# A hybrid decoder step on one core: the closing stage of each 512-token segment gets a rank 800 operations later

## The chip, the core and the metric

The kernel runs on one core of a Trainium2 chip. A core has a matrix engine (TensorE, PE), a vector engine (VectorE, DVE), a scalar engine (ScalarE, ACT), a general engine (GpSimd, POOL) and a queue engine (SyncE, SP). Each works through its own list of instructions in order. Instructions of different engines wait for each other by semaphores. The metric is the device time of one execution in microseconds (us), the median of several runs.

## The reference

One layer of a causal decoder runs over a prompt of 2048 tokens (width 1024) and over a sample batch of 8 sequences of 4 tokens. In short:

```
u    = x * (1 + scale) + shift                 # from the conditioning vector
proj = u @ w_in                                # 9344 columns
A    = rwkv7(proj)                             # 16 heads of 64: a delta-rule recurrence
B    = retention(proj)                         # 4 heads, chunks of 128 tokens
merged = sigmoid(g_a) * o_a + sigmoid(g_b) * o_b
sub  = merged @ w_out
y    = norm(alpha * x + gate * sub) * ln_gain + ln_bias
```

The last line is the closing stage that the change moves.

## The kernel before, in words

The prompt is cut into four segments of 512 tokens. In each segment the kernel goes over four retention heads, and with each head over two pairs of recurrence heads. `run` records the work of a head by a list of steps (`ORDER`): `P0` and `P1` are the projections of a pair, `G0` and `G1` the gate projections, `R` the projections and `S` the arithmetic of the retention head, `J` prepares half a pair and runs `solve`, `N` and `M` merge, `O` is the output projection of the head before, and `D` is the decode of the sample batch, which runs once, in segment 2. A projection is 24 matmuls of 128 x 512 into a PSUM tile `pp` (three of them). Its weights are a 1 MB tile `ww` (three of them), a high and a low part side by side, which POOL loads from a copy in DRAM (`wc_wf`) that segment 0 wrote. `solve` is a chain: it inverts a matrix in six levels (DVE writes `HH` and two copies `bdH`, PE multiplies), and then walks four chunks of the recurrence.

The step `O` of a segment's first head also closes the segment before: its fourth head is projected, and then `final` runs on the finished tile `zt` (128 x 4 x 1024, one buffer). `final` is 76 operations: for each of two column halves a DMA of the gate row and for each of four row blocks a DMA of x, a POOL multiplication by the gate, a DVE addition and a DVE statistic; then the row statistics (a POOL power among them); then for each half two DMAs (gain and bias rows) and for each block a DVE normalization, a POOL multiplication, a DVE addition and the DMA to the output. Its DMAs are issued by SP into four `fx` tiles. The last segment does not come here (`outproj_last`), so `final` runs three times for the prompt, in segments 1, 2 and 3. A fourth call, for the sample batch, is small and stands elsewhere.

Nothing of this is issued as recorded. `Plan` records every operation with a number, finds what each depends on, and `schedule` then plays the whole list through a cost model of the five engines: at each step the engine that is free first takes, of its operations that are ready, the one with the lowest rank. The rank is the recorded number plus an offset that holds while the operation is recorded:

```
op.num = len(self.ops)
op.prio = op.num + self.prio_off
```

PE chooses among ranks less than 500 apart (`WIN`); weights tiles keep their order. An operation is never held back for its rank: where an engine has nothing else ready, it takes it. The first work of a segment (`uprep`) already has an offset, -700. The result is a fixed list for each engine.

All instructions of the trace carry line 529, where recorded operations are issued, so they are told apart by tile names.

Of the kernel before, what the change touches and what calls it, by code (L numbers as in the profile page):

```python
# [62 lines left out]
RUN = 2  # L63
UPO = 700
DOFF = 0
JBN = 3, 2, 2, 2, 2
JB=dict(zip(("AR", "W", "UV", "BT", "Z"), JBN))
NPP,NSM = 3,3
# [758 lines left out]
class Mixer:  # L827
# [980 lines left out]
    def outproj(self, s, h, dec):  # L1808
        T, V, A, G = self.T, self.V, self.A, self.G
        last = s == self.ns - 1  # L1810
        if last and h == NH_B - 1:
            return self.outproj_last(s)
        if h == 0:
            self.zt = self.j1.tile([128, 4, D], F32, tag="zt", name="zt")
        for q in range(4):
            qs = slice(q * 256, (q + 1) * 256)
            if last:
                if q % 2 == 0:
                    wg = self.ww.tile([128, 2, 2, 512], F32R, tag="ww", name="ww")
                hi, lo = self.split(self.i["wo"][h, q], wg[:, q % 2, 0], wg[:, q % 2, 1], gate=q)  # L1820
            else:
                if q % 2 == 0:
                    wp = self.wpair("wo", (h, q), [self.i["wo"][h, q + g] for g in range(2)], s < self.ns - 2)
                hi, lo = wp[q % 2]
            ws = [slice(k * 256, (k + 1) * 256) for k in range(2)]
            for i2 in range(2):
                pz = self.pp.tile([128, 2, 256], F32, tag="pp", name="pp")
                for j in range(2):
                    i = i2 * 2 + j
                    n = 0  # L1830
                    for k in (1, 0):
                        mh, ml = self.mg[k]
                        for w, m in ((hi, mh), (hi, ml), (lo, mh)):
                            T.matmul(pz[:, j], lhsT=m[:, i * 128:(i + 1) * 128], rhs=w[:, ws[k]], start=n == 0, stop=n == 5)
                            n += 1
                z = self.zt[:, 2 * i2:2 * i2 + 2, qs]
                if h == 0 and last:
                    x = self.fx((128, 2, 256))
                    r = s * SEG + i2 * 256
                    self.nc.sync.dma_start(out=x, in_=self.i["xp"][r:r + 256, qs].rearrange("(j p) c -> p j c", j=2))  # L1840
                    V.scalar_tensor_tensor(out=z, in0=x, scalar=ALPHA, in1=pz, op0=MUL, op1=ADD)
                elif h == 0:
                    A.copy(out=z, in_=pz)
                else:
                    V.tensor_tensor(out=z, in0=pz, in1=z, op=ADD)
            if dec:
                self.outproj_dec(h, [(q, (hi, lo))])
        self.mg = {}
        if h == NH_B - 1:
            rows = [slice(s * SEG + i * 128, s * SEG + (i + 1) * 128) for i in range(4)]  # L1850
            self.final([[self.zt[:, i, 0:512], self.zt[:, i, 512:1024]] for i in range(4)], 128,
                       [self.i["xp"][r] for r in rows], [self.o["yp"][r] for r in rows], False)

    def outproj_last(self, s):

# [108 lines left out]
    def run(self):  # L1964
# [3 lines left out]
        for s in range(self.ns):  # L1968
# [8 lines left out]
            for h in range(NH_B):  # L1977
                last = s == self.ns - 1 and h == NH_B - 1
                gate = {}
                for step in (LAST if last else ORDER if s + h else BEGIN).split():  # L1980
# [28 lines left out]
                    elif step[0] == "D" and s == self.dseg + 1 and h == 0:  # L2009
                        self.pl.prio_off = DOFF  # L2010
                        self.decode()
# [28 lines left out]
```

## Time and profile before

| what | value |
| --- | --- |
| median of 3 runs | 3134.05 us (3130.12 to 3137.01) |
| the profiled execution, its own time | 3128.51 us |
| its span, first to last instruction | 3126.7 us |
| PE busy | 2896.4 us, 93% of the span |
| DVE, ACT, POOL busy | 61%, 50%, 34% |
| mean granted PE clock | 0.969 of full |

The profiled execution lies 5.5 us under the median. PE is the engine that is busy nearly all the time, so the end of the program moves by what PE waits, by what its clock loses, and by little else. A row of the timeline gives the start, the length, the engine, the operation, out<-in by names, the shape and a count of equal instructions in a row; in brackets stands how long the engine was idle before, and what ended that.

### The profile page before, as it was taken

Reading aid. Unit: us, or ns where it says so; the run is one execution under the profiler, and the core shown is the slowest. Engines: PE = TensorE matmul, PEld = TensorE weight load, DVE = VectorE, ACT = ScalarE, POOL = GpSimd, SP = SyncE. Lnnn points to the kernel's source line nnn. Section 1 sums busy time; section 2 is a strip of 40 time slices with the busy share of each in tenths; the row PEclk is TensorE's granted clock in tenths of the full one; section 3 lists DMA queues with packets and bytes.
Section 4 is the critical chain, followed back from the end, with each engine's and each line's share of the span. In section 5 each row is a group of like instructions: output and inputs, shape, how many; then the busy total and the mean of one; then the engine's idle time right before and its main releaser. Section 6 shows DMA issues by size and latency. Waiting matters only on the chain. (4 is left out here: it accounts for less than half of the span.)

```text
span 3126.7 us, 63842 instructions
## 1 busy us (share of the span) xinstructions
PE 2896.4 (93%) x24700; PEld 2332.8 (75%) x24700; DVE 1919.9 (61%) x4748; ACT 1566.2 (50%) x3859; POOL 1048.3 (34%) x1451
## 2 busy tenths in 40 slices
PE   8999999989989999989998788999999989998996
PEld 5777778768888989879774466777787766777675
DVE  3566676666576365565665575565676675566666
ACT  4466755656436455453541045554555346454652
POOL 4554456433252131222210242232232442334232
PEclk9999999999999999999998789999999999999997
DMA  8564556534362433425344432333343452533321
GB/s 303 199 229 161 175 191 222 191 127 160 117 226 99 130 108 112 137 94 178 136 128 150 158 110 97 135 124 122 131 152 124 156 176 79 172 119 122 108 83 38
DMA packets 132792, 451.86 MB, mean 145 GB/s; under 512 B 30500, under 2 KB 41636, under 8 KB 92680
## 3 DMA queue, kind: packets, MB, share of 16 engines
q0 software_dynamic: 33120, 241.19, 22.5%
q1 hardware_dynamic: 99368, 206.58, 19.6%
q8 instruction: 195, 3.19, 0.4%
q14 instruction: 109, 0.89, 0.1%
HBM read 345.83 MB, written 101.88 MB: 143 GB/s over the span
## 5 line engine op out<-in xcount | busy, mean ns | idle before, releaser
L529 PE MATMUL pp<-uh,ww 128*128 128x512 f32 (+1 forms) x5152 | 1476.8, 366 | 43.8 <-DMA ww<-wc_wf 15.6
L529 PEld LDWEIGHTS pp<-uh,ww 128*128 128x128 f32 x5152 | 880.5, 190 | 168.3 <-DVE t L529 22.7
L529 PE MATMUL pp<-ul,ww 128*128 128x512 f32 (+1 forms) x2576 | 883.7, 364 | 0.1
L529 PEld LDWEIGHTS pp<-ul,ww 128*128 128x128 f32 x2576 | 468.6, 190 | 54.5 <-issue 1.4
L529 POOL DMA_DIRECT2D ww<-wc_wf x190 | 109.0, 574 | 625.3 <-PE pp L529 514.5
L529 POOL TENSOR_TENSOR ww<-fx,ww 128x512 fp32r<-128x512 f32 x178 | 234.4, 1330 | 211.5 <-ACT ww L529 197.7
L529 ACT CAST ZX<-sm 128x512 f16<-128x512 f32 (+1 forms) x363 | 206.3, 572 | 91.0 <-PE sm L529 86.7
L529 ACT ACTIVATE tn<-UV,PL 64x64 f32<-64x64 f32 x512 | 177.0, 346 | 117.9 <-DVE UV L529 95.8
L529 POOL TENSOR_TENSOR t<-t,t 128x256 fp32r<-128x256 f32 (+2 forms) x160 | 150.6, 943 | 199.5 <-ACT t L529 189.1
L529 DVE TENSOR_TENSOR HH<-sm,lev 128x512 f16<-128x512 f32 (+1 forms) x165 | 111.3, 674 | 160.5 <-PE sm L529 159.7
L529 PE MATMUL pp<-ww,mh 128*128 128x256 f32 x960 | 190.4, 290 | 3.5 <-ACT zt L529 1.9
L529 DVE TENSOR_SCALAR UV<-ch 64x64 f32<-64x64 f32 x256 | 55.2, 227 | 207.3 <-ACT UV L529 184.4
L529 POOL TENSOR_TENSOR tn<-tn,mhalf 128x4 f32<-128x4 f32 (+2 forms) x108 | 100.9, 935 | 216.1 <-DVE tn L529 214.1
L529 PE MATMUL pp<-ww,uh 128*128 128x256 f32 x1024 | 171.6, 291 | 1.4 <-DVE t L529 0.8
L529 ACT CAST bdZ<-sm 64x512 f16<-64x512 f32 (+1 forms) x264 | 149.5, 566 | 24.9 <-PE sm L529 20.1
L529 PEld LDWEIGHTS pp<-ww,mh 128*128 128x128 f32 x960 | 154.9, 193 | 8.0 <-ACT zt L529 2.3
L529 PEld LDWEIGHTS pp<-ww,uh 128*128 128x128 f32 x1024 | 140.7, 190 | 5.3 <-ACT UV L529 0.7
L529 DVE SCALAR_TENSOR_TENSOR UV<-ch,PL,tn 64x64 f32<-64x64 f32 x384 | 108.7, 283 | 57.4 <-PE ch L529 47.5
L529 ACT ACTIVATE t<-pp 128x512 f32<-128x512 f32 (+1 forms) x160 | 80.6, 519 | 118.3 <-PE pp L529 100.7
L529 PE MATMUL pp<-ww,ml 128*128 128x256 f32 x480 | 138.4, 289 | 0.1
L529 ACT ACTIVATE UV<-ch 64x64 f32<-64x64 f32 x256 | 51.6, 215 | 171.3 <-PE yy L529 137.8
L529 DVE COPY bdH<-HH 64x512 f16<-64x512 f16 (+1 forms) x396 | 124.7, 315 | 8.5
(255 smaller groups left out, 5420.1 us busy)
## 6 DMA issues: line engine op xcount, KB each, us to landing
ww<-wc_wf POOLq DMA_DIRECT2D x190, 1024.0 KB, 5.1
wc_wf<-ww SPq DMA_DIRECT2D x65, 1024.0 KB, 5.4
fx<-in_wf SPq DMA_DIRECT2D x140, 256.0 KB, 3.4
ww<-wc_wv POOLq DMA_DIRECT2D x24, 1024.0 KB, 5.2
ww<-wc_wo POOLq DMA_DIRECT2D x16, 1024.0 KB, 5.1
wa<-in_wa SPq DMA_DIRECT2D x16, 512.0 KB, 5.2
wc_wv<-ww SPq DMA_DIRECT2D x8, 1024.0 KB, 5.5
fx<-in_wo SPq DMA_DIRECT2D x32, 256.0 KB, 2.8
```

What stands on the lines that cost most here:

```text
L529: op.fn = lambda: real(*[res(x) for x in a], **{k: res(x) for k, x in kw.items()})
```

## The change

The three calls of `final` for the prompt are recorded with an offset of +800, so each of their operations ranks like one recorded 800 operations later. The operations themselves, their tiles and what they depend on stay as they are.

```diff
@@ -63,6 +63,7 @@
 RUN = 2
 UPO = 700
 DOFF = 0
+FOFF = 800
 JBN = 3, 2, 2, 2, 2
@@ -1848,8 +1849,10 @@
         self.mg = {}
         if h == NH_B - 1:
             rows = [slice(s * SEG + i * 128, s * SEG + (i + 1) * 128) for i in range(4)]
+            off, self.pl.prio_off = self.pl.prio_off, FOFF
             self.final([[self.zt[:, i, 0:512], self.zt[:, i, 512:1024]] for i in range(4)], 128,
                        [self.i["xp"][r] for r in rows], [self.o["yp"][r] for r in rows], False)
+            self.pl.prio_off = off
```

Recorded 800 operations later stand the rest of the first head's steps (`G1`, `S`, `J`, `M`) and the first steps of the second head. The lists of the five engines are the same before and after up to each `final`, differ for some 200 to 350 us of work around it, and are the same again before the next one. The added line moves every line number by one.

On DVE in segment 1, after the statistics of `final`. Before, the rows with `zt` and `fx` or `tn` are `final`; `AR` and `BK` are a pair's preparation, and `t<-pp,omu,t` empties a projection's PSUM tile:

```order
L529 TENSOR_TENSOR AR<-t_10662,t_11273 128x4x64
L529 TENSOR_SCALAR zt<-zt,tn 128x512 x3
L529 TENSOR_TENSOR zt<-zt,fx 128x512 x3
L529 TENSOR_SCALAR zt<-zt,tn 128x512 x3
L529 TENSOR_TENSOR zt<-zt,fx 128x512 x3
L529 TENSOR_SCALAR zt<-zt,tn 128x512 x2
L529 TENSOR_TENSOR AR<-t_10575,t_11273 128x4x64
L529 SCALAR_TENSOR_TENSOR t_11409<-pp,omu,t_11342 128x256 x2
```

After, the same stretch, from the same first row to the emptying of the same tile:

```order
L530 TENSOR_TENSOR AR<-t_10662,t_11293 128x4x64
L530 BN_STATS tn<-zt 128x6
L530 BN_AGGR tn<-tn 128x2
L530 TENSOR_TENSOR AR<-t_10575,t_11293 128x4x64
L530 SCALAR_TENSOR_TENSOR t_11340<-t_11213,t_10662 128x256
L530 BN_AGGR tn<-tn 128x2
L530 SCALAR_TENSOR_TENSOR t_11351<-t_11232,t_10662 128x256
L530 SCALAR_TENSOR_TENSOR BK<-t_11340,t_11298 64x4x64 x2
L530 SCALAR_TENSOR_TENSOR t_11382<-pp,omu,t_11337 128x256 x2
```

Fourteen rows' worth of normalizations and additions stood between the two `AR` and ahead of the emptying; now three short statistics stand there.

On POOL in segment 2, behind the decode. Before; `lw` is the pair of small weights that the next pair's first matmuls read, and `zt<-zt,fx` are `final`'s gate multiplications:

```order
L529 DMA ww<-wc_wv_0_2375 128x2048
L529 TENSOR_TENSOR zt<-zt,fx 128x512 x4
L529 COPY PL<-t_22078 128x4
L529 TENSOR_SCALAR t_22113<-t_22016 128x4x64
L529 TENSOR_SCALAR t_22122<-t_22017,hka,oka 128x256
L529 MEMSET t_22113 128x4
L529 TENSOR_TENSOR t_22122<-t_22122,t_20456 128x256
L529 TENSOR_TENSOR lw<-t_22084,lw 128x256
```

After:

```order
L530 TENSOR_TENSOR t_22014<-t_22014,t_20456 128x256
L530 TENSOR_TENSOR zt<-zt,fx 128x512
L530 TENSOR_TENSOR tn<-tn,mhalf 128x2
L530 COPY PL<-t_22054 128x4
L530 TENSOR_TENSOR lw<-t_21992,lw 128x256
L530 TENSOR_TENSOR tn<-tn,mhalf 128x2
L530 TENSOR_SCALAR t_22091<-t_22060 128x4x64
```

`lw` now stands ahead of the second half's four multiplications and of the other half pair's operations, with one multiplication in front of it.

On POOL in segment 3, where it issues the loads of projection weights (`DMA ww<-wc_wf`, the number names the block). Before:

```order
L529 DMA ww<-wc_wf_2062 128x2048
L529 TENSOR_TENSOR tn<-tn,mhalf 128x4
L529 TENSOR_TENSOR zt<-zt,fx 128x512 x3
L529 COPY t_30476<-carry 128x1
L529 COPY t_30510<-carry 128x1
L529 COPY carry<-t_30476 128x1
L529 COPY carry<-t_30510 128x1
L529 TENSOR_TENSOR zt<-zt,fx 128x512 x4
L529 DMA ww<-wc_wf_2131 128x2048
L529 DMA ww<-wc_wf_2170 128x2048
```

After:

```order
L530 DMA ww<-wc_wf_2062 128x2048
L530 TENSOR_TENSOR zt<-zt,fx 128x512 x3
L530 TENSOR_TENSOR t_30469<-t_30392,t_30460 128x256
L530 COPY t_30473<-carry 128x1
L530 DMA ww<-wc_wf_2131 128x2048
L530 TENSOR_TENSOR bdL<-W,B_29946 64x4x64 x2
L530 TENSOR_SCALAR t_30515<-t_30490 128x4x64
```

Between the loads of blocks 2062 and 2131 stood seven multiplications and the power (`tn<-tn,mhalf`, which waits for the row statistics); now three multiplications of the first pass stand there.

## Rows read from the trace of the kernel before

**Rows 1.** The page: span, and busy time by engine

```profile
span 3126.7 us, 63842 instructions
PE 2896.4 (93%) x24700; PEld 2332.8 (75%) x24700; DVE 1919.9 (61%) x4748; ACT 1566.2 (50%) x3859; POOL 1048.3 (34%) x1451
```

**Rows 2.** Instructions on the tile zt: count, ns min/median/max, first and last start

```profile
L529 POOL TENSOR_TENSOR zt<-zt,fx x48: 1257/1461/2487, 876.1 to 2521.0; 128x512 f32<-128x512 f32 x48
L529 DVE BATCH_NORM_STATS2 tn<-zt x32: 632/682/695, 878.8 to 3117.2; 128x6 f32<-128x512 f32 x32
...
L529 DVE SCALAR_TENSOR_TENSOR zt<-fx,zt x24: 633/692/1780, 877.4 to 2501.5; 128x512 f32<-128x512 f32 x24
L529 DVE TENSOR_SCALAR zt<-zt,tn x24: 529/663/1519, 900.2 to 2520.4; 128x512 f32<-128x512 f32 x24
L529 DVE TENSOR_TENSOR zt<-zt,fx x24: 678/1384/1785, 903.0 to 2523.7; 128x512 f32<-128x512 f32 x24
```

**Rows 3.** Stretches: length, busy PE, PEld, DVE, ACT, POOL, clock, DMA share, GB/s

```profile
890.00:921.00 31.00, 19.09 (x136) 18.70 (x137) 29.11 (x46) 7.35 (x21) 24.03 (x27) 0.83 0.68 237
921.00:970.00 49.00, 46.02 (x542) 41.23 (x542) 30.94 (x75) 30.23 (x77) 10.99 (x18) 1.00 0.43 144
...
1784.00:1831.00 47.00, 27.25 (x143) 20.74 (x141) 40.85 (x66) 14.56 (x28) 35.87 (x36) 0.75 0.52 167
1831.00:1880.00 49.00, 45.01 (x470) 35.91 (x467) 28.74 (x86) 30.69 (x81) 9.17 (x16) 0.97 0.28 97
...
2471.00:2527.00 56.00, 41.60 (x197) 33.87 (x195) 45.35 (x65) 8.81 (x18) 37.73 (x39) 0.92 0.69 224
2527.00:2580.00 53.00, 50.90 (x502) 41.77 (x502) 31.27 (x69) 28.08 (x61) 11.51 (x18) 0.96 0.42 149
```

**Rows 4.** Timeline of PE: its long waits in the three stretches

```profile
917.04 0.59 PE L529 MATMUL pp<-uh,ww 128*128 128x272 f32 x1 [10.23 <-DVE t L529]
...
1787.20 0.39 PE L529 MATMUL sm<-lora,lw 128*128 128x256 f32 x1 [2.60 <-ACT lw L529]
1795.92 1.01 PE L529 MATMUL sm<-lora,lw 128*128 128x256 f32 x3 [8.33 <-POOL lw L529]
...
1818.15 0.73 PE L529 MATMUL pp<-uh,ww 128*128 128x512 f32 x1 [5.00 <-DVE gate_t L529]
...
2491.25 0.77 PE L529 MATMUL pp<-uh,ww 128*128 128x512 f32 x1 [3.45 <-DMA ww<-wc_wf]
...
2526.93 0.77 PE L529 MATMUL pp<-uh,ww 128*128 128x512 f32 x1 [9.33 <-DMA ww<-wc_wf]
```

**Rows 5.** Timeline of DVE in segment 1; last row: inside a solve

```profile
899.61 0.41 DVE L529 TENSOR_TENSOR AR<-t,t 128x256 f32<-128x256 f32 x1
900.25 2.66 DVE L529 TENSOR_SCALAR zt<-zt,tn 128x512 f32<-128x512 f32 x3 [0.23 <-POOL tn L529]
...
915.10 1.48 DVE L529 TENSOR_TENSOR AR<-t,t 128x256 f32<-128x256 f32 x1
916.51 1.26 DVE L529 SCALAR_TENSOR_TENSOR t<-pp,omu,t 128x256 f32<-128x256 f32 x3
...
942.32 0.69 DVE L529 TENSOR_TENSOR HH<-sm,lev 128x512 f16<-128x512 f32 x1 [1.34 <-PE sm L529]
```

**Rows 6.** Timeline of POOL in segments 2 and 3

```profile
1785.56 6.85 POOL L529 TENSOR_TENSOR zt<-zt,fx 128x512 f32<-128x512 f32 x4
...
1794.69 1.17 POOL L529 TENSOR_TENSOR lw<-t,lw 128x256 fp32r<-128x256 f32 x1
...
2476.85 6.14 POOL L529 TENSOR_TENSOR zt<-zt,fx 128x512 f32<-128x512 f32 x4 [3.87 <-DMA fx<-gdram]
...
2512.62 6.07 POOL L529 TENSOR_TENSOR zt<-zt,fx 128x512 f32<-128x512 f32 x4
2518.64 1.71 POOL L529 DMA_DIRECT2D ww<-wc_wf  x3
```

**Rows 7.** Stretch behind the first long wait, columns as in rows 3

```profile
917.00:921.00 4.00, 3.96 (x19) 3.96 (x20) 3.91 (x10) 1.63 (x2) 1.31 (x2) 0.56 0.48 145
```

## The prediction

> **What bounds the kernel now.** I read the page first: PE is busy for 2896.4 of 3126.7 us, so 230 us of idle PE are all that an order of work can win back, apart from its clock [rows 1]. The reader is to see there which engine decides, and that the others have room on average. Then I looked for where `final` runs, by its tile [rows 2]: 48 POOL multiplications are three stages of 16, and the 24 of each kind on DVE are three times 8. By medians a stage is 16 x 1.46 = 23.4 us of POOL and 8 x (0.69 + 0.66 + 1.38 + 0.68) = 27.3 us of DVE, with five small DVE instructions more. Third, the stretches in which it runs [rows 3]: there DVE is busy for 29.11 of 31, 40.85 of 47 and 45.35 of 56 us, and PE stands idle for 11.9, 19.8 and 14.4 us, 46 us together. In the stretches right behind them DVE has 18.1, 20.3 and 21.7 us free and PE idles for only 3.0, 4.0 and 2.1 us. So the average of 61% for DVE hides three places where DVE and POOL are the bound, and there the last thing that PE waits for is read one wait at a time [rows 4].
>
> **The waits, each with what stood ahead of its releaser.** In segment 1 PE waits 10.23 us for `t`, the emptying of a PSUM tile. DVE reaches it at 916.51; from 900.25 to 915.10 it runs fourteen instructions of `final`, then one `AR` [rows 5]. In segment 2 PE waits 2.60 us for one half of `lw`, 8.33 us for the other and 5.00 us for `gate_t`, another emptying [rows 4]. POOL writes `lw` at 1794.69, behind four multiplications that begin at 1785.56 and take 6.85 us and behind a few instructions of the pair [rows 6]; `gate_t` stands behind instructions of `final` on DVE in the same way. In segment 3 PE waits 3.45 and 9.33 us for weights [rows 4]. Their loads are issued by POOL in its order: the load that PE lacks at 2526.93 is one of three issued at 2518.64, right behind four multiplications of 6.07 us, and the earlier one stood behind four of 6.14 us which had themselves waited 3.87 us for the gate row [rows 6]. Sum of the six waits: 10.23 + 2.60 + 8.33 + 5.00 + 3.45 + 9.33 = 38.9 us.
>
> **The change part by part.** It adds and removes no instruction; it moves three times 76.
>
> First, what leaves its place ahead of the releasers. The order shows it at each of them. In segment 1 the emptying has no normalization ahead of it any more. PE had stopped 10.23 us before 917.04, so at 906.8; without the fourteen instructions DVE, at 900 where it was before, has the statistics, one `AR`, two short products and two `BK` to do, an estimate of 3.5 us if each takes up to twice the 0.41 us of the `AR` [rows 5], and reaches the emptying before PE needs it. I take the whole 10.2 us. In segment 2 `lw` has one multiplication ahead of it in place of four and no longer the other half pair, and no instruction of the additions of `final` stands ahead of `gate_t`. I take 8.3 + 5.0 us as gone, and leave the 2.6 us, since what PE comes to next there (transposes of the retention output) waits for a POOL power and four DVE instructions; since that may cost 1.4 us more, I count 12 us. In segment 3 the load of block 2131 has three multiplications (4.4 us) ahead of it in place of seven and a power. PE does not outrun that by more than a little, so I leave 2 us and count 10.8 us. Together 10.2 + 12 + 10.8 = 33 us. The bounds are 0, if other work on the same engines is as late, and 46 us, the whole idle time of the stretches.
>
> Second, the clock. After the wait of 10.23 us PE runs for 4 us at a mean clock of 0.56, so at the lower of its two levels, 1.2 of 2.4 GHz, for most of it, and loses 3.96 x 0.44 = 1.7 us [rows 7]. Three of the waits are of this kind, one in each segment, so 5 us come back with them; bounds 0 and 10.
>
> Third, what is given back where the 76 operations go. The normalizations now stand between the instructions of `solve`: by the order, 14 of the 37 DVE instructions of the first stage, 31 of the second and 29 of the third stand behind the start of the first solve. That is 74 x (27.3 / 37 = 0.74) = 55 us, against 60 us of free DVE in the three stretches behind [rows 3]. Where DVE waits for PE between two levels, 1.34 us, one of them fits without delay [rows 5]; where it falls between `HH` and its copies it lengthens the chain by its own 0.7 to 1.4 us. The cover is PE's own projection matmuls, which fill the chain's gaps (3 us idle of 49 in such a stretch [rows 3]); if that cover is gone, the chain's delay is PE's. The bounds are 0 and 55. I take 8 us: about a third of the 55 us on the chain, and less than half of that seen by PE. The solve itself also begins earlier, because the `AR` and `BK` that it needs are no longer behind `final`, which speaks for the lower end.
>
> Fourth, the rest. SP issues the same 22 DMAs a stage in nearly the same places, so its queue is not moved past anything that PE reads. The `fx` tiles are held longer, but no other user of them is near; the one `zt` is wanted again only by the second head's output projection. On both I put 0 to 3 us and take 0. The rows of the lists that differ elsewhere are neighbours exchanged; 0 with 4 us to either side.
>
> Sum: 3128.5 - 33 - 5 + 8 = 3098.5 us against the profiled execution's own time. This lies 5.5 us under the median of the runs, so the median I predict is 3104 us, 30 us less than before.
>
> One row and one rule speak against it. `AR<-t,t` took 0.41 us at 899.61, and 1.48 us at 915.10 with a multiplication of POOL beside it [rows 5]; `zt<-zt,fx` on DVE goes from 0.68 to 1.79 us [rows 2]. The Trainium skill (SBUF — State Buffer, section Who interferes with whom) says that a VectorE instruction with two inputs in SBUF, or a copy in a two-port mode, and a GpSimd instruction exclude each other for the whole instruction, whichever came first. By it the multiplications, now among the copies of the solve, would each hold one link of the chain for 1.46 us; the trace agrees as far as these two rows go. That is the first rival.
>
> **The rivals.**
> 1. The shared access gives back half. With about ten of the 16 multiplications of each stage behind the start of a solve, 30 x 1.46 = 44 us can fall on links of the chain; if half does and PE sees half again to two thirds of it, 11 to 15 us come back beyond my 8, and the time is 3115 to 3127 us. For it: the stretched rows above. Against it: in the old place the two engines met too, 29 of 31 us busy DVE beside 24 us of POOL [rows 3].
> 2. The waits only change their name: PE lacks PSUM tiles or weights for another reason at the same place, such as the pair's own chain behind the decode, and 3134 us stay, within 6 us. For it: the stretch behind the decode has a low clock, 0.75 [rows 3], so PE is short of work there. Against it: in segments 1 and 3 there is nothing else between the releaser and its data.
> 3. Slower: the solve chain becomes PE's bound. Its place is the first solve behind each stage, its price the 55 us of DVE instructions now inside. It decides from the point where PE sees more than 38 of them, that is when the projections run out in all three solves; with all 55 seen, the time is 3134 + 17 = 3151 us. For it: 31 and 29 of 37 instructions stand there. Against it: 60 us of free DVE, and the schedule's preference for the chain wherever both are ready.
>
> **How the numbers follow.** The forecast, 3092 to 3116 us: 0.62. A gain beyond it, when the solves' earlier start counts too: 0.08. Rival 1: 0.17. Rival 2: 0.06. Rival 3: 0.07. What a measurement of this kernel can tell from no change is about 0.2%, 6 us: faster 0.62 + 0.08 + 0.17 = 0.87, the same 0.06, slower 0.07. The range from 3087 to 3127 holds the forecast, rival 1 and half of the larger gain, about 8 in 10; its upper end is where the gain ends, its lower end has nearly all 46 us of idle time gone.
>
> **What would show it.** In the new profile no wait of PE over 4 us should stand in the three stretches, with at most 3 us left of the one for `lw`; the clock should stay at 1.00 in segment 1; DVE should be busy for over 80% in the solves behind, with `zt` rows between `HH` and `bdH`, and PE idle there by 2 to 4 us more than before. Long waits of `ch` or `sm` matmuls for `UV`, `HH` or `bdH` in those solves would show rival 3, stretched `bdH` copies rival 1, and a wait of 8 us or more left at any of the three places would prove the first step wrong.

## The result and the profile after

The changed kernel takes 3097.3 us (median of 4 executions, 3090.48 to 3099.47) against 3134.44 us: a ratio of 0.9879 with a 95% interval of 0.986 to 0.9898. It is 37 us faster. The forecast was 3104 us and the range 3087 to 3127. The profiled execution took 3099.47 us, 29 us less than that of before.

The page after, answering to [rows 1]. The engines work as long as before; the idle time of PE fell from 230 to 200 us:

```profile
span 3097.7 us, 63856 instructions
PE 2897.5 (94%) x24700; PEld 2331.9 (75%) x24700; DVE 1913.9 (62%) x4748; ACT 1567.7 (51%) x3859; POOL 1040.3 (34%) x1451
```

The three stages and the solves behind them, answering to [rows 3], same columns. The first of each pair is the stage, the second the solve. These are stretches of time: each pair holds 4 to 11% more matmuls than its pair of before, the stage of segment 1 alone 242 in place of 136:

```profile
889.00:920.00 31.00, 29.06 (x242) 27.98 (x242) 24.84 (x48) 12.81 (x39) 17.38 (x31) 1.00 0.63 207
920.00:969.00 49.00, 41.80 (x514) 37.17 (x512) 37.47 (x79) 26.65 (x66) 14.29 (x15) 1.00 0.45 150
1780.00:1810.00 30.00, 26.62 (x163) 21.34 (x163) 25.18 (x42) 12.72 (x26) 18.88 (x26) 0.89 0.32 103
1810.00:1860.00 50.00, 47.47 (x474) 37.11 (x473) 41.87 (x109) 30.16 (x80) 22.52 (x28) 1.00 0.63 207
2451.00:2503.00 52.00, 45.48 (x263) 36.90 (x262) 36.21 (x58) 14.78 (x30) 25.21 (x37) 0.93 0.60 203
2503.00:2551.00 48.00, 44.91 (x464) 35.74 (x460) 44.47 (x102) 22.52 (x57) 21.61 (x22) 1.00 0.60 201
```

Length less busy PE is PE's idle time: in the stages 1.9, 3.4 and 6.5 us where it was 11.9, 19.8 and 14.4; in the solves 7.2, 2.5 and 3.1 where it was 3.0, 4.0 and 2.1. Cut at the same number of matmuls instead, the stages lose 9.4, 16.9 and 7.9 us of idle time, 34.2 us together by either way. VectorE has become fuller in the solves (37.47 of 49, 41.87 of 50, 44.47 of 48 us) and emptier in the stages.

The long waits of PE, answering to [rows 4]. The emptying in segment 1 is still waited for, 1.52 us in place of 10.23; no wait for `lw` over 0.42 us nor for a weights load of `wc_wf` is left in these stretches; two new ones are for `BK`, a product of a pair's preparation on VectorE (the first of them lies 6 us behind the end of segment 2's solve stretch):

```profile
906.76 0.40 PE L530 MATMUL pp<-uh,ww 128*128 128x272 f32 x1 [1.52 <-DVE t L530]
...
1865.91 1.09 PE L530 MATMUL sm<-cst,BK 128*128 128x128 f32 x4 [4.25 <-DVE BK L530]
...
2484.52 1.12 PE L530 MATMUL sm<-cst,BK 128*128 128x128 f32 x4 [6.52 <-DVE BK L530]
```

**A ledger by matmuls.** Since both kernels issue the same matmuls, the program can be cut at the same ones (the counts agree to one record). Five cuts, before:

```profile
849.59:1245.00 395.41, 372.23 (x3684) 345.51 (x3684) 239.57 (x611) 197.34 (x544) 121.60 (x182) 0.99 0.39 132
1698.65:1775.97 77.32, 62.02 (x188) 30.03 (x188) 34.42 (x89) 5.34 (x17) 5.75 (x8) 0.65 0.40 138
1775.97:1969.93 193.96, 162.23 (x1329) 127.67 (x1328) 128.40 (x305) 93.48 (x225) 69.78 (x90) 0.93 0.35 117
2299.99:2475.20 175.21, 169.49 (x1404) 132.45 (x1404) 115.41 (x294) 92.56 (x218) 52.59 (x85) 1.00 0.43 143
2475.20:2699.93 224.73, 199.26 (x1498) 157.16 (x1498) 142.56 (x324) 96.73 (x231) 92.85 (x122) 0.95 0.45 154
```

The same after:

```profile
848.77:1237.28 388.51, 370.05 (x3685) 344.27 (x3684) 238.56 (x611) 198.44 (x544) 120.56 (x182) 1.00 0.40 134
1691.24:1773.47 82.23, 67.86 (x187) 32.11 (x188) 34.48 (x89) 5.42 (x17) 5.41 (x7) 0.59 0.39 129
1773.47:1945.05 171.58, 158.63 (x1329) 126.15 (x1328) 122.44 (x304) 92.15 (x224) 64.89 (x90) 0.96 0.39 132
2274.70:2455.02 180.32, 172.82 (x1405) 135.67 (x1404) 115.04 (x293) 93.69 (x219) 50.85 (x84) 0.98 0.40 137
2455.02:2668.65 213.63, 196.83 (x1499) 154.34 (x1497) 144.39 (x324) 96.19 (x231) 91.39 (x123) 0.98 0.49 163
```

| cut | length | idle PE | rest (clock) |
| --- | --- | --- | --- |
| segment 1, stage and solves | -6.9 | -4.7 | -2.2 |
| decode, order unchanged | +4.9 | -0.9 | +5.8 |
| segment 2, stage and solves | -22.4 | -18.8 | -3.6 |
| ahead of segment 3's stage | +5.1 | +1.8 | +3.3 |
| segment 3, stage and solves | -11.1 | -8.7 | -2.4 |

The last column is the first less the second: what PE took longer or shorter for the same matmuls, its clock above all. The three stages give 40.4 us; 5.1 are lost ahead of the third, where the order has a few exchanged neighbours, and 4.9 in the decode, where the order is that of before. With 1.4 us elsewhere this makes the 29 us.

### The profile page after: what moved, and what is told of

Same layout as the page of the kernel before. It is cut to its first block, busy times and chain, and to the rows that moved or that the text cites. A ratio compares the mean times of both kernels' runs of the same rounds, so it can differ in the third digit from the quotient of the medians.

```text
span 3097.7 us, 63856 instructions
## 1 busy us (share of the span) xinstructions
PE 2897.5 (94%) x24700; PEld 2331.9 (75%) x24700; DVE 1913.9 (62%) x4748; ACT 1567.7 (51%) x3859; POOL 1040.3 (34%) x1451
## 5 line engine op out<-in xcount | busy, mean ns | idle before, releaser
L530 PE MATMUL pp<-uh,ww 128*128 128x512 f32 (+1 forms) x5152 | 1479.1, 366 | 14.5 <-DVE t L530 4.8
```

The lines of the kernel that those rows point to most:

```text
L530: op.fn = lambda: real(*[res(x) for x in a], **{k: res(x) for k, x in kw.items()})
```

## The experiments

Times are medians. The kernel before took 3134.44 us beside the changed kernel; 3135.75 beside the three with one call and the one with the second pass only; 3135.26 beside rank 400, rank 1600, the multiplications on VectorE and the kernel with segment 2 whole at 1600; and 3134.45 beside the other three. The last four columns are the change of length of segment 1's cut, segment 2's, the one ahead of segment 3 and segment 3's (to 2852 us of before), each against the profile of before. Each is read from one profile, and the same lists do not always take equally long: in segment 3 the two profiles of the changed kernel differ by 4.4 us, and three kernels with the same lists there (second pass only, and that with segment 2 whole at 1600 or its first pass at 400) by 3.6 us. So differences of some 4 us between rows of that column tell nothing.

| kernel | us | ratio, 95% interval | seg. 1 | seg. 2 | ahead | seg. 3 |
| --- | --- | --- | --- | --- | --- | --- |
| changed | 3097.3 | 0.9879, 0.986 to 0.9898 | -6.9 | -22.4 | +5.1 | -11.1 |
| changed, again | 3096.0 | 0.9872, 0.9857 to 0.9886 | -8.1 | -22.4 | +3.2 | -15.5 |
| first call only | 3127.75 | 0.9979, 0.9967 to 0.9991 | -8.6 | +1.2 | -0.4 | -1.4 |
| second call only | 3134.0 | 0.9996, 0.9984 to 1.0008 | +1.1 | -23.1 | +3.3 | +17.8 |
| third call only | 3118.1 | 0.9954, 0.9936 to 0.9972 | +0.3 | +0.9 | -1.7 | -15.9 |
| second pass only | 3089.1 | 0.9858, 0.9837 to 0.9879 | -11.4 | -9.8 | -0.4 | -23.7 |
| rank 400 | 3101.3 | 0.989, 0.9872 to 0.9908 | -6.8 | -12.8 | -0.2 | -16.4 |
| rank 1600 | 3096.5 | 0.9873, 0.9855 to 0.989 | -11.2 | -12.5 | -0.1 | -12.5 |
| multiplications on VectorE | 3101.0 | 0.9893, 0.9877 to 0.9908 | +4.8 | -15.2 | -0.3 | -19.6 |
| second pass, segment 2 whole at 1600 | 3088.7 | 0.9852, 0.9838 to 0.9867 | -12.6 | -12.3 | +0.6 | -20.1 |
| second pass at 1600 | 3111.6 | 0.9924, 0.991 to 0.9937 | -11.6 | -0.1 | -0.1 | -8.3 |
| second pass, segment 2's first at 400 | 3081.8 | 0.983, 0.9817 to 0.9844 | -12.5 | -15.3 | -0.5 | -20.4 |

**One call at a time.** The condition is `s == 0`, `s == 1` or `s == 2`:

```diff
-            off, self.pl.prio_off = self.pl.prio_off, FOFF
+            off, self.pl.prio_off = self.pl.prio_off, FOFF if s == 0 else 0
```

> Only the first of the three calls of `final` is ranked 800 later; its order is that of the changed kernel from 884 to 1241 us and that of the kernel before everywhere else. Theory A (each stage gives its own share, and the shares add up): the same matmul ends 6.8 us earlier behind this stretch in the changed kernel's trace (5 us less idle PE, 2 us of clock), so 3127.5 us, 3124 to 3131. Theory B (the gain of the first stage is given back in its solve, which idles for 7.2 of 49 us instead of 3.0): 3131 to 3134 us.

> Only the second call is ranked later. Theory A: 22.4 us are gained from 1783 to 1964 us, as in the changed kernel's trace, and some 7 us lost between 2306 and 2437, where this kernel has the same exchanged neighbours as the changed one: 3119 us, 3114 to 3123. Theory B (the loss there was one execution's chance and not the order's): 3112 us.

> Only the third call is ranked later; up to 2478 us its order is that of the kernel before, so the exchanged neighbours ahead of it (2306 to 2437) are not there. Theory A (the 7.8 us lost in that stretch by the changed kernel come from the exchange alone): the 14.1 us of the stage itself remain, 3120 us, 3116 to 3124. Theory B (the loss belongs to the stage, its work only pushed forward): 6 us, 3128 us.

The first and the third came as theory A has it (3127.75 and 3118.1 us). The third shows that the stage's gain does not need the loss ahead of it: where the neighbours are not exchanged, that cut is not longer. The second call fell outside both theories: its own stage gave 23.1 us, as in the changed kernel, the 3.3 us ahead of segment 3 were lost too, and then segment 3, whose `final` kept its old rank, took 17.8 us more. PE in that stretch, two long waits:

```profile
2501.82 0.76 PE L530 MATMUL pp<-uh,ww 128*128 128x512 f32 x1 [8.84 <-DVE zt L530]
2519.07 0.50 PE L530 MATMUL pp<-uh,ww 128*128 128x512 f32 x1 [3.59 <-DVE gate_t L530]
```

POOL ahead of the first:

```profile
2485.15 5.70 POOL L530 TENSOR_TENSOR zt<-zt,fx 128x512 f32<-128x512 f32 x4 [8.50 <-DMA fx<-gdram]
...
2493.43 0.61 POOL L530 DMA_DIRECT2D ww<-wc_wf  x1
```

The profile puts the first wait down to an addition of `final` (`zt`), since one ended just then, but a projection's matmul does not read `zt`. It reads `ww`: the load issued at 2493.43 landed at 2501.69, 0.13 us before the matmul, and 0.14 us lie between landing and matmul in both waits for loads of [rows 4]. So it is a weights load again, on POOL behind four multiplications that had themselves waited 8.50 us for the gate row. The second wait is for an emptying behind instructions of `final` on VectorE.

And the solve that comes later, in the columns of [rows 3]:

```profile
2612.00:2650.00 38.00, 24.01 (x309) 18.33 (x308) 16.48 (x59) 19.32 (x50) 1.23 (x2) 0.64 0.00 1
```

Here PE has almost no projection left to put between the links of the chain: 14 of its 309 matmuls write a `pp`, no weights arrive (DMA share 0.00), PE idles for 14 of 38 us, and the clock is 0.64. This is the mechanism of the prediction's third rival, in another place than it expected. So the three gains do not add up, 8 + 1.8 + 17.7 us against 37 to 38 together: what segment 2 gives, segment 3 takes back unless its `final` is moved as well.

**The second pass alone.** Offset only from the row statistics on:

```diff
-            off, self.pl.prio_off = self.pl.prio_off, FOFF
+            off = self.pl.prio_off
...
+        self.pl.prio_off += 0 if dec else FOFF
         for i in range(n):
             V.bn_aggr(out=mv[:, 2 * i:2 * i + 2], in_=st[:, i * 12:i * 12 + 12])
```

> In all three calls the first pass (gate multiplication on POOL, residual and statistics on DVE) keeps its rank, and only the second pass (normalization, gain, bias, store) is ranked 800 later. Theory A (what PE lacks stands behind different halves: the emptying in segment 1 behind the second pass on DVE, `lw` in segment 2 behind the first pass on POOL, the loads in segment 3 behind the multiplications of both): segment 1 gains its 7 us, segment 2 the 5.0 us of `gate_t` but not the 8.33 of `lw`, segment 3 about half of 14; 3115 us, 3108 to 3122, and in the trace a wait of PE of 5 us or more for `lw` is left. Theory B (the second pass is the whole burden): 3097 to 3103 us and no such wait.

Its time, 3089.1 us, is below both theories, but the trace has the wait that theory A named, behind the first pass on POOL. PE:

```profile
1792.00 1.01 PE L530 MATMUL sm<-lora,lw 128*128 128x256 f32 x3 [8.48 <-POOL lw L530]
```

POOL, with the four multiplications first:

```profile
1781.50 6.42 POOL L530 TENSOR_TENSOR zt<-zt,fx 128x512 f32<-128x512 f32 x4
...
1790.69 1.26 POOL L530 TENSOR_TENSOR lw<-t,lw 128x256 fp32r<-128x256 f32 x1
```

Segment 1 gained 11.4 us with the first pass in place, so there the second pass alone was the burden. Segment 3 gained 23.7 us, 14.5 of them idle PE; the rest is what PE takes for its matmuls, its clock above all. The two kernels below that have the same lists there gained 20.1 and 20.4 us, so some 20 us are the order's. Which of its exchanged rows does that was not tried out. A wait of 4.78 us for a weights load is left in segment 3.

**The size of the offset.**

```diff
-FOFF = 800
+FOFF = 400
```

> The changed kernel with 400 in place of 800. Theory A (the rank only has to carry `final` behind the releasers that PE lacks; how far beyond does not matter): all three stage gains stay, and since up to 2482 us segment 3 has the order of the kernel before, without the exchanged neighbours, the 5 to 7 us lost there are saved: 3092 us, 3086 to 3098. Theory B (400 is short of the releasers, part of `final` is ahead of them still): waits of PE of 4 us or more for `lw`, `t` or the loads are left, 3105 to 3120 us.

> The changed kernel with 1600 in place of 800. Theory A (as above, it is free behind the releasers; no exchanged neighbours ahead of segment 3 here either): 3092 us, 3086 to 3098. Theory B (the normalizations fall deeper into the solves, each of them on the chain of VectorE, and PE sees them): the stretches behind the stages idle for 3 us more each than in the changed kernel, 3105 to 3112 us.

Both have the cut ahead of segment 3 at its old length, as expected, and neither is faster for it: 3101.3 us, between the two theories (one wait of 5.09 us for a load is left in segment 3), and 3096.5 us, in theory A's range. Their segment 2 gives 12.8 and 12.5 us where 800 gives 22.4. So the offset is not free behind the releasers; each value leads to another order in the solves, and in segment 2 these differ by 10 us.

**The multiplications of `final` on VectorE.**

```diff
-                G.tensor_tensor(out=z, in0=z, in1=gate[0:P], op=MUL)
+                (G if dec else V).tensor_tensor(out=z, in0=z, in1=gate[0:P], op=MUL)
...
-                G.tensor_tensor(out=z, in0=z, in1=g[0:P], op=MUL)
+                (G if dec else V).tensor_tensor(out=z, in0=z, in1=g[0:P], op=MUL)
```

> The changed kernel (800) with the 48 prompt multiplications of `final` on VectorE in place of GpSimd. Theory A (the shared access costs the changed kernel its rest: PE waits 6.52 us for `BK` in segment 3, whose two products took 4.57 us beside 3.70 us of GpSimd multiplications, against 0.42 us each elsewhere): no wait of PE for `BK` over 3 us, no `zt`, `BK` or `bdH` row stretched beyond twice its usual time, GpSimd 65 us less busy; VectorE's own 16 x 0.68 = 11 us a stage fit: 3090 us, 3084 to 3096. Theory B (the stretching is off the path that matters, and VectorE is the fuller engine in the stages): 3100 to 3115 us.

Theory B: 3101.0 us, not faster than the changed kernel. Its page, against that of the changed kernel:

```profile
PE 2901.9 (94%) x24700; PEld 2334.6 (75%) x24700; DVE 1914.5 (62%) x4796; ACT 1565.8 (50%) x3859; POOL 978.7 (32%) x1403
```

VectorE has 48 instructions more, of 0.685 us in the median, so 33 us, and yet the same busy time: by this difference, an estimate, about 33 us of its time in the changed kernel is standing beside GpSimd. In the places of the two long waits for `BK` none is left, the sign of theory A. But no time comes of it. The solve behind segment 1's stage now idles for 12 of 49 us at a clock of 0.79:

```profile
921.00:970.00 49.00, 36.97 (x433) 31.50 (x432) 35.77 (x100) 30.45 (x74) 6.56 (x11) 0.79 0.36 120
```

**The changed kernel again, and two combinations.** The combinations take an offset for each pass and segment: `((0, 1600, 0), (800, 1600, 800))`, then `((0, 0, 0), (1600, 1600, 1600))` and `((0, 400, 0), (800, 800, 800))`, first pass first:

```diff
-            off, self.pl.prio_off = self.pl.prio_off, FOFF
+            off, self.pl.prio_off = self.pl.prio_off, FOFF[0][s]
+            self.foff2 = FOFF[1][s]
...
+        if not dec:
+            self.pl.prio_off = self.foff2
         for i in range(n):
             V.bn_aggr(out=mv[:, 2 * i:2 * i + 2], in_=st[:, i * 12:i * 12 + 12])
```

> The changed kernel a second time, to tell what its order does from what one execution does. Theory A (the order does it): 3097 us, 3092 to 3101; in its trace again 4 us or more more idle PE and 5 us or more in all lost between 2306 and 2437 us of the kernel before, waits of PE for `BK` of 4 us and over in segments 2 and 3, and a clock below 0.62 in the decode. Theory B (chance): at least the loss or one of the two waits is absent, and the time nearer 3090 us.

The time is theory A's, 3096.0 us; of its signs the clock in the decode (0.59) and the wait of 4.24 us in segment 2 came again, the loss ahead of segment 3 with 3.2 us and 1.5 us of idle PE only in part, and the wait for `BK` in segment 3 was 2.47 us in place of 6.52. That one of the two waits falls short was named under theory B: in this part it was chance. Why that one varies is seen on VectorE in the first trace:

```profile
2475.88 0.69 DVE L530 SCALAR_TENSOR_TENSOR zt<-fx,zt 128x512 f32<-128x512 f32 x1 [4.26 <-DMA fx<-in_xp]
2476.49 0.42 DVE L530 TENSOR_TENSOR AR<-t,t 128x256 f32<-128x256 f32 x1
...
2479.90 4.57 DVE L530 TENSOR_TENSOR BK<-t,t 64x256 f32<-64x256 f32 x2
```

VectorE stood 4.26 us for a row of x, ahead of the `AR` and `BK` that PE needed. In the second trace this row has no such wait in front of it; what stays is the stretched pair of `BK`:

```profile
2471.00 0.69 DVE L530 SCALAR_TENSOR_TENSOR zt<-fx,zt 128x512 f32<-128x512 f32 x1
...
2475.16 4.50 DVE L530 TENSOR_TENSOR BK<-t,t 64x256 f32<-64x256 f32 x2
```

Beside it on POOL:

```profile
2475.19 3.75 POOL L530 TENSOR_TENSOR zt<-zt,fx 128x512 f32<-128x512 f32 x3
```

> Second pass ranked 800 later in segments 1 and 3 with the first pass in place, as in the kernel with the second pass alone; in segment 2 the whole of `final` is ranked 1600 later. Theory A (the wait of 8.48 us for `lw` that the second pass alone leaves in segment 2 stands behind the first pass, and is worth its length plus the clock behind it): no such wait, 3079 us, 3074 to 3084. Theory B (segment 2 gives its gain back in segment 3, as it did when it was ranked later alone): 3086 to 3092 us.

> The second pass of all three calls ranked 1600 later in place of 800, the first pass in place. Theory A (behind the releasers the rank is free): 3089 us, 3085 to 3093. Theory B (the second pass at 800 has 24 us from segment 3, 9 of them by the clock, through an order that differs up to 2851 us; at 1600 it differs only up to 2646, as in the kernels whose segment 3 gained 10 to 14 us): 3096 to 3101 us.

> The second pass ranked 800 later in all three calls, and the first pass 400 later in segment 2 alone. Theory A (the wait for `lw`, 8.48 us, goes, and nothing else changes, since the order outside 1776 to 1964 us is that of the second pass alone): 3081 us, 3077 to 3085. Theory B (its place in segment 2 is taken by waits in the solves behind, as at 1600, where 8 us came and 8 went): 3086 to 3091 us.

The first has the time of theory B, 3088.7 us, but its reason is not shown: the lists of segment 3 are those of the second pass alone, and the 3.6 us less that it gains there are no more than the same lists vary. The wait for `lw` is gone, and segment 2's cut itself is only 2.5 us shorter than with the second pass alone; waits of 3.80, 2.53 and 2.99 us stand in its solves. The second is worse than either theory, 3111.6 us: the wait for `lw` is 9.37 us there, and a solve in segment 2 idles for 9 of 30 us. The third has the time of theory A, within a microsecond, and is the fastest of all: 3081.8 us. That closeness is in part luck. Against the second pass alone the profiled execution is 8.0 us shorter, and the ledger gives 5.5 us of that to segment 2; the decode, whose list is the same, took 4.1 us less, and segment 3, also with the same lists, 3.3 us more. So the wait of 8.48 us was worth 5.5 us in these profiles. None of the second half's four multiplications stands ahead of `lw` any more, which is written at 1774.06; the last of the first half's four stands at 1770.03, and no wait for `lw` is left:

```profile
1770.03 1.28 POOL L530 TENSOR_TENSOR zt<-zt,fx 128x512 f32<-128x512 f32 x1
...
1774.06 0.91 POOL L530 TENSOR_TENSOR lw<-t,lw 128x256 fp32r<-128x256 f32 x1
```

## Why the prediction was right

**The waits that go: right, 34 us for 33.** By stage the idle time fell by 10.0, 16.4 and 7.9 us where 10.2, 12 and 10.8 were counted. In segment 2 the 2.60 us for the first half of `lw` went too, and the fear that its place would be taken there did not come true. In segment 3 the loads are no longer waited for, as forecast, but 6.52 us for `BK` stand in their place; that no wait over 4 us would remain was wrong. The operations that were named as standing ahead of the releasers are the right ones: with the first pass left in place in segment 2 the wait for `lw` comes back at 8.48 us, and it goes again when only that pass is moved; in segment 1 no wait of PE over 2.4 us is left when only the second pass is moved.

**The clock: right in its direction, too small.** In the three stage cuts it gives 2.2 + 3.6 + 2.4 = 8.2 us, 5 forecast with bounds of 0 and 10. Places where the forecast took nothing take it back in this pair of profiles: 3.3 us ahead of segment 3 and 5.8 in the decode. In segment 1 the granted clock is 1.00, as forecast.

**What is given back in the solves: smaller than the 8 us taken.** The stages lost 34.2 us of idle time and the three cuts together 32.2, so 2 us came back: 5.3 in segment 1 and less than nothing in the other two. In the second profile of the changed kernel the three cuts lost 38.5 us, much of the difference being the shorter wait for `BK`. VectorE is busy for 76, 84 and 93% of the solves (over 80% forecast, missed in segment 1), and PE idles there by 4.2 us more, 1.5 less and 1.0 more than before (2 to 4 more forecast). VectorE's additions and normalizations cost less in their new place. The tile's rows, answering to [rows 2]:

```profile
L530 POOL TENSOR_TENSOR zt<-zt,fx x48: 1255/1294/1656, 875.3 to 2534.8; 128x512 f32<-128x512 f32 x48
...
L530 DVE TENSOR_SCALAR zt<-zt,tn x24: 540/547/3309, 909.6 to 2534.1; 128x512 f32<-128x512 f32 x24
L530 DVE TENSOR_TENSOR zt<-zt,fx x24: 659/686/2152, 913.4 to 2538.1; 128x512 f32<-128x512 f32 x24
```

The medians went from 663 to 547 and from 1384 to 686 ns, so a stage's 27.3 us were an overestimate for the place they were moved to: before, they were measured where they stood in a row beside the multiplications.

**The neighbours exchanged elsewhere: 0 was wrong, and the bound of 4 us was passed once.** Ahead of segment 3 they cost 5.1 and 3.2 us in the two profiles of the changed kernel and 3.3 with the second call alone; in the other nine this cut is between 1.7 us shorter and 0.6 longer than before. The lists of segment 3 are not the same as before up to its `final`, as was said with the change: they differ from 2306 us of before on, 170 us ahead of the first multiplication of `final` at 2477. This comes with the second call's offset of 800, since the second call alone has it and the third alone has not. That it costs the time is an association over twelve profiles; a kernel with that exchange alone was not tried.

**The sum: nearer than its terms.** The sum gave 3098.5 us for the profiled execution, and 3099.47 was measured. That is luck. The gain was forecast too small by 1.2 us in the waits, 3.2 in the clock and 6.0 in what is given back, 10.4 together; and 5.1 us ahead of segment 3 (taken as 0), 4.9 in the decode and 1.4 elsewhere (no term), 11.4 together, were lost again.

**From the profile to the median: a term that did not hold.** The 5.5 us that were added for the median did not carry over: the changed kernel's profiled execution lies 2 us above its median. The profile of before had a quick decode, 77.3 us at a clock of 0.65; with the order of the decode unchanged, eleven of the twelve later profiles take 4.7 to 6.9 us more there. So the 29 us between the two profiles are too small a measure: with the decodes equal they are 34, which is nearer to the 37 between the medians. Only the fastest kernel's profile has a quick decode too, 1.2 us over that of before; whether its other executions had one is not known.

**The rivals.** The first, the shared access, is real and small. `BK` waits out three multiplications in both traces, at 3.7 us (4.50 to 4.57 us for two of 0.42), but the copies `bdH`, named as the sign, took 1594 ns at most, against 1380 before. The Trainium skill (SBUF — State Buffer, section Who interferes with whom) says that a VectorE instruction with two inputs in SBUF contends with a GpSimd instruction that reads it, and these rows agree. But spread out, the two engines meet less often than in a row: by the medians above the interference of `final` itself fell, and taking the multiplications off GpSimd gained nothing. Its range was also wider than its sum: 11 to 15 us beyond 3104 end at 3119, not at 3127. The second, waits that only change their name, is true at one of the three places, of `BK` in segment 3. The other wait for `BK`, 4.25 and 4.24 us in the two traces, stands behind segment 2's solve; VectorE has no row of `final` in the 9 us ahead of that `BK`, and its cause is open. The third, a solve without cover, did not decide here: the solves idle for 3 to 7 us, and the longest wait for one of its named tiles is 1.63 us, for `HH`. It did with the second call alone, where it helped to eat a gain of 23 us.

## What to carry to other kernels

When the work of a closing stage stands ahead of what the busiest engine waits for, read at each such wait which instructions of the stage precede its releaser and on which queue; rank only those behind it, and for each place by itself: the best of the orders tried this way took 3081.8 us here in place of 3134.4, against 3097.3 for one offset on all. The sizes of the offsets were found by trying: the second pass at 1600 in place of 800 gave 3111.6. In a list made by a scheduler an offset is not a dial: 400, 800 and 1600 differ by what the order does to later work, so judge it by a ledger between equal matmuls over the whole program, not by the stage. Compare medians with medians, and ask whether a stretch that did not change took equally long in the two profiles before a difference is explained.

## What was not expected of the hardware

One VectorE instruction can stand through several GpSimd instructions, not only one. One `BK` with a median of 421 ns took 4134 ns beside three multiplications of `zt` in a row, and 4060 ns in the second trace; a normalization whose median is 547 ns took 3309 ns, beside a load's issue and two multiplications. The longest of GpSimd's multiplications of `zt` is 1656 ns. By the recorded starts, which are rough on GpSimd, the two `BK` began 0.15 and 0.03 us before the first of the three, so these rows do not show that the one that comes first goes first.

The granted clock over the same list of the decode was 0.65 and 0.64 in two of the thirteen profiles and 0.59 to 0.61 in the other eleven. Between the profile of before and that of the changed kernel PE was busy 5.8 us longer for it, with less idle time beside it (15.3 and 14.4 us). What decides it is not shown.
